# One pass per tile, or three phases over all tiles: reordering an encoder layer with streamed weights

## The chip, the cores and the metric

The kernel runs on all 8 cores of one Trainium2 chip (two dies of four cores). Every core runs the same program on its own share of the data, and no core waits for another. The time of a run is the device time of the slowest core, in microseconds (us). A trace covers one execution; its "span" is the time from a core's first to its last instruction, and the page of a kernel shows its slowest core.

Executions come in two states. In the fast state all cores have nearly the same granted TensorE clock (in the fast runs of the changed kernel, 0.987 to 0.992). In the slow state the cores of one die, sometimes of both, have a lower clock and run longer: where a kernel gave fast runs too, its slow runs in a batch are 1.8 to 17% above the fastest of them. Fast runs are compared with fast runs only; where a kernel gave none, an undisturbed die is compared with an undisturbed die, and the text says so.

Engine names: PE is the matrix engine, PEld its weight load (it overlaps PE: in a window of 100 us of before, 45.32 us of it with PE busy for 99.88), DVE the vector engine, ACT the scalar engine, SP the engine that issues most transfers. "L414" is line 414 of the kernel that is being shown; the line numbers of an experiment can be one off from those of the kernel it was made from.

## The reference, cut to what matters

```python
D_MODEL, D_FF, BATCH, SEQ = 1024, 2816, 16, 2048     # 2 prompt sequences per core
DEC_BATCH, DEC_SEQ = 8, 64                            # 1 sample of 64 tokens per core

def encoder_layer(x, cache_k, cache_v, state_gla, ...):
    h = x + 0.5 * swiglu_ffn(rms_norm(x, norm_ffn1), w_ffn1_in, w_ffn1_out)      # FFN 1
    n = rms_norm(h, norm_mix)
    q_a, k_a, v_a, r_a, f_a, q_b, k_b, v_b, g_a, g_b = split_projection(n, w_in)
    o_a, s_new = gla_branch(q_a, k_a, v_a, r_a, f_a, ...)     # 4 heads, recurrent over chunks of 64
    o_b = band_attention(q_b, k_b, v_b, ...)                  # 16 heads of 64, own chunk + 8 before
    mixed = sigmoid(g_a) * (o_a @ w_branch_gla) + sigmoid(g_b) * (o_b @ w_branch_att)
    h = h + mixed @ w_out
    h = h + 0.5 * swiglu_ffn(rms_norm(h, norm_ffn2), w_ffn2_in, w_ffn2_out)      # FFN 2
    return h, ...                                             # and the new keys, values, GLA state
```

All weights come in as fp32 and are used as bf16. Both kernels cut a core's 4096 prompt tokens into 8 tiles of 512. Each tile needs the GLA state and the last 512 keys and values of the tile before it in its sequence. The sample tile (64 tokens) starts from given caches.

## The kernel before

It takes one tile through the whole layer, then the next; the sample is the last tile. All weights are first cast from fp32 to bf16 by transfers from HBM to HBM (`wsc`), and every tile streams them from there in 1 MB blocks through a ring of three slots.

```python
if not ws.planning and not DIRECT0:                       # at the start: cast all blocks HBM -> HBM
    for j in range(ws.nbt):
        ...
            S.op("pool", (lambda e, d=dst_j, s_=src_j: e.dma_start(out=d, in_=s_)), writes=[("wsc", j)], dma=True)
...
# getw(): a tile's next block of weights, 2 blocks ahead, for every tile anew
S.op("sp", (lambda e, slot=slot, jb=jb, n_el=n_el: e.dma_start(out=ring[:, slot, 0:n_el], in_=wsc[jb][:, 0:n_el])),
     reads=[("wsc", jb)], writes=[("wring", slot)], dma=True)
```

The order of instructions is the order in which the code emits them. In a tile: FFN 1, norm with transposes, projections, GLA, attention, gates and output, norm, FFN 2. Attention takes a head's scores (five matmuls of 64 rows by 128 columns), adds the bias, takes exp, and multiplies by the values (five matmuls of 65 columns); scores of the next head fill PE while ACT and DVE work on this one, and nothing else does.

```python
ins = e.matmul(outp, lhsT=kbT[pb0:pb0 + 64, c, sl * 128:sl * 128 + nk],             # L875, scores
               rhs=qbT[pb0:pb0 + 64, c, s * 128:s * 128 + TP], start=True, stop=True)
... # L881 bias add on DVE; L889 and L895 exp on ACT
ins = e.matmul(acc[:TP, acol:acol + 65], lhsT=Pb[:nk, pbuf, i, 0:TP], rhs=vaug[:nk, sl, hd, :],   # L921, times values
               start=(n_ == 0), stop=(n_ == len(blks) - 1))
...
for q in range(NSEQ):
    for t in range(NT):
        tile("p", q, t)
tile("s", 0, 0)
```

The code makes two readers of one PSUM bank wait for each other (`if kname(r) == "ps": war.add(rd)`). The changed kernel keeps that rule, so it is not part of the difference.

The softmax here doesn't subtract the row's maximum and nothing guards it: scores larger than these inputs give would overflow.

Of the kernel before, what the change touches and what calls it, by code (L numbers as in the profile page):

```python
# [6 lines left out]
F32 = mybir.dt.float32  # L7
# [6 lines left out]
PW = 8208  # L14
EPS = 1e-6
NCORES = 8

COMPUTE = ("pe", "act", "dve")
QUEUES = ("sp", "pool")
NDMASEM = 12  # L20

OVERLAPS = {
    "gT": ["ebT", "enbT", "la", "oaT", "obT", "qdT", "kiT"],
    "ebT": ["gT", "oaT"], "oaT": ["gT", "ebT"],
    "enbT": ["gT", "obT"], "obT": ["gT", "enbT"],
    "la": ["gT", "qdT", "kiT"], "qdT": ["gT", "la"], "kiT": ["gT", "la"],
    "dke": ["oa", "h2"], "oa": ["dke", "h2"], "va": ["ob", "h2"], "ob": ["va", "h2"], "h2": ["dke", "oa", "va", "ob"],
    "hout": ["rr", "qbT"], "rr": ["hout"], "qbT": ["hout"],
    "Pb": ["Pbg"], "Pbg": ["Pb"],
}  # L30

def kname(k):
    return k[0] if isinstance(k, tuple) else k

class Sched:
    def __init__(self):
        self.ops = []
        self.last_w = {}
        self.readers = {}
        self.nseq = {e: 0 for e in COMPUTE + QUEUES}  # L40
        self.pending = {}

    def enter(self, name):
        deps = set()
        others = set(OVERLAPS[name])
        for k, v in self.last_w.items():
            if kname(k) in others:
                deps.add(v)
        for k, v in self.readers.items():
            if kname(k) in others:  # L50
                deps.update(v)
        best = {}
        keep = set()
        for d in deps:
            o = self.ops[d]
            if o["dma"]:
                keep.add(d)
            else:
                if o["eng"] not in best or self.ops[best[o["eng"]]]["seq"] < o["seq"]:
                    best[o["eng"]] = d  # L60
        keep.update(best.values())
        self.pending[name] = keep

    def op(self, eng, fn, reads=(), writes=(), dma=False):
        idx = len(self.ops)
        raw = set()
        war = set()
        for r in reads:
            if r in self.last_w:
                raw.add(self.last_w[r])  # L70
            if kname(r) == "ps":
                for rd in self.readers.get(r, ()):
                    war.add(rd)
        for w in writes:
            if w in self.last_w:
                raw.add(self.last_w[w])
            for rd in self.readers.get(w, ()):
                war.add(rd)
            p = self.pending.get(kname(w))
            if p:  # L80
                raw.update(p)
        for r in reads:
            self.readers.setdefault(r, []).append(idx)
        for w in writes:
            self.last_w[w] = idx
            self.readers[w] = []
        seq = self.nseq[eng]
        self.nseq[eng] += 1
        self.ops.append(dict(eng=eng, fn=fn, raw=raw, war=war - raw, dma=dma, seq=seq,
                             sig=False, waits=[], idx=idx))  # L90
        return idx

    def barrier(self, eng, deps):
        idx = len(self.ops)
        seq = self.nseq[eng]
        self.nseq[eng] += 1
        self.ops.append(dict(eng=eng, fn=None, raw=set(deps), war=set(), dma=False, seq=seq,
                             sig=False, waits=[], idx=idx))
        return idx

    def analyze(self):
        ops = self.ops
        seen = {e: {x: -1 for x in COMPUTE} for e in COMPUTE + QUEUES}
        seen_dma = {e: set() for e in COMPUTE + QUEUES}
        dma_count = {q: 0 for q in QUEUES}
        dma_hist = {q: [] for q in QUEUES}
        for o in ops:
            e = o["eng"]
            deps = [(d, True) for d in sorted(o["raw"])] + [(d, False) for d in sorted(o["war"])]
            if o["dma"]:  # L110
                n = dma_count[e]
                dma_count[e] += 1
                o["dsem"] = n % NDMASEM
                o["dval"] = 16 * (n // NDMASEM + 1)
                if n >= NDMASEM:
                    deps.append((dma_hist[e][n - NDMASEM], True))
                dma_hist[e].append(o["idx"])
            for d, is_raw in deps:
                a = ops[d]
                if a["dma"]:  # L120
                    if d in seen_dma[e]:
                        continue
                    o["waits"].append(d)
                    seen_dma[e].add(d)
                else:
                    ae = a["eng"]
                    if a["fn"] is None:
                        continue
                    if ae == e and ae == "pe":
                        continue  # L130
                    if seen[e][ae] >= a["seq"]:
                        continue
                    o["waits"].append(d)
                    a["sig"] = True
                for x in COMPUTE:
                    if a["vc"][x] > seen[e][x]:
                        seen[e][x] = a["vc"][x]
            vc = dict(seen[e])
            if e in COMPUTE:
                vc[e] = o["seq"]  # L140
            o["vc"] = vc
        cnt = {e: 0 for e in COMPUTE}
        for o in ops:
            if o["eng"] in COMPUTE and o["sig"]:
                cnt[o["eng"]] += 1
                o["sval"] = cnt[o["eng"]]

    def emit(self, sems, dsems, block):
        ops = self.ops
        per = {e: [o for o in ops if o["eng"] == e] for e in COMPUTE + QUEUES}  # L150

        def run(engname, eng):
            for o in per[engname]:
                for d in o["waits"]:
                    a = ops[d]
                    if a["dma"]:
                        eng.wait_ge(dsems[a["eng"]][a["dsem"]], a["dval"])
                    else:
                        eng.wait_ge(sems[a["eng"]], a["sval"])
                if o["fn"] is None:  # L160
                    continue
                ins = o["fn"](eng)
                if o["dma"]:
                    ins.then_inc(dsems[engname][o["dsem"]], 16)
                elif o["sig"]:
                    ins.then_inc(sems[engname], 1)

        block.tensor(lambda eng: run("pe", eng))
        block.scalar(lambda eng: run("act", eng))
        block.vector(lambda eng: run("dve", eng))  # L170
        block.gpsimd(lambda eng: run("pool", eng))
        block.sync(lambda eng: run("sp", eng))

class NullSched:
    def op(self, *a, **k):
        return 0

    def enter(self, name):
        pass

NSLOT = 3
LOOKAHEAD = 2
DIRECT0 = False

class WStream:
    def __init__(self, ring):
        self.ring = ring
        self.plan = []
        self.rearr = []
        self.planning = True  # L190
        self.issued = 0
        self.taken = 0
        self.S = None

    def view(self, slot, shape):
        a, b = shape
        return self.ring[:, slot, 0:a * b].rearrange("p (a b) -> p a b", a=a)

class StopEmit(Exception):
    pass  # L200

def build(NSEQ, SEQLEN, debug=(), stop_at=None):
    nc = bass.Bass("TRN2", target_bir_lowering=False)
    NTOK = NSEQ * SEQLEN
    NT = SEQLEN // 512

    def din(name, shape, dt=F32):
        return nc.dram_tensor(name, shape, dt, kind="ExternalInput").ap()

    def dout(name, shape):  # L210
        return nc.dram_tensor(name, shape, F32, kind="ExternalOutput").ap()

    def dscr(name, shape):
        return nc.dram_tensor(name, shape, BF16, kind="Internal").ap()

    xp = din("xp", [NTOK, D])
    xsm = din("xs", [64, D])
    ck = din("ck", [512, D])
    cv = din("cv", [512, D])
    st = din("st", [4, 128, 256])  # L220
    wsrc = dict(
        w1i=din("w1i", [D, 2 * DFF]), w1o=din("w1o", [DFF, D]), win=din("win", [D, PW]),
# [3 lines left out]
    gnf_d = din("gnf", [1, D])  # L226
    biasT_d = din("biasT", [128, 16, 2, 128])
    cb_d = din("cb", [128, 16])
    consts_d = din("consts", [128, 4, 128])

    yp = dout("yp", [NTOK, D])
    ys = dout("ys", [64, D])
# [953 lines left out]
```

## Time and profile before

| before | value | where read |
|---|---|---|
| time, 3 runs | 5112.84 us median (5000.71 to 5132.51; two of the three are over 2% above the fastest) | runs |
| span, slowest core | 4992.2 us | page |
| PE / DVE / ACT busy | 84% / 29% / 29% | page |
| dense stage | 216 ns per matmul of 512 columns (464 in 100.32 us), clock 1.00 | chain of waits, windows |
| attention stage | 74 us per tile, clock 0.50 | windows |
| a prompt tile | 526 to 591 us | first FFN 1 activation of each tile |
| sample tile | about 240 us (232.6 from its first activation to the end) | the same, to the end |

The lines of the page of before. First busy time with share of the span and number of instructions; then 40 equal slices of the span, each digit the busy share in tenths ("PEclk" is the granted clock in tenths); then the chain of work that ended last, by engine.

```profile
span 4992.2 us, 66123 instructions; the slowest of 8 cores (4942.5 to 4992.2 us)
PE 4201.9 (84%) x22747; PEld 2087.6 (42%) x22747; DVE 1450.3 (29%) x2982; ACT 1444.3 (29%) x2840; POOL 138.9 (3%) x205
...
PE   4646776998999899988999799989999899969956
...
PEclk8778678996999689996999799987999699977975
DMA  9999899430443134330443134322342044322586
...
PE 66%; DMA 14%; another core or an unknown queue 6%; DVE 5%; issue 4%; ACT 3%; POOL 1%; DVEq 0%; ACTq 0%; POOLq 0%; SPq 0%
```

PE looks busy, but PEclk is below 9 in 19 of the 40 slices: at the start, and then once or twice per tile. The first seven slices (the casting) have DMA at 8 tenths or more and PE at 4 to 7 tenths.

Windows of before, core 7: a dense stage and the attention stage of the same tile. Columns are the window, its length, busy time and count per engine, then granted clock, DMA share, GB/s.

```profile
core 7: us, PE busy (x) PEld busy (x) DVE busy (x) ACT busy (x) POOL busy (x), PEclk, DMA share, GB/s
1442.00:1542.00 100.00, 99.88 (x463) 45.32 (x464) 23.87 (x35) 14.99 (x25) 4.32 (x8) 1.00 0.51 174
1688.00:1762.00 74.00, 67.85 (x657) 49.12 (x656) 42.28 (x153) 60.35 (x129) 0.00 (x0) 0.50 0.01 2
```

A line of the chain of waits of before: 464 dense matmuls back to back, 216 ns each.

```profile
1442.12 100.32 PE ps L414 x464
```

### The profile page before, as it was taken

Reading aid. Unit: us, or ns where it says so; the run is one execution under the profiler, and the core shown is the slowest. Engines: PE = TensorE matmul, PEld = TensorE weight load, DVE = VectorE, ACT = ScalarE, POOL = GpSimd, SP = SyncE. Lnnn points to the kernel's source line nnn. Section 1 sums busy time; section 2 is a strip of 40 time slices with the busy share of each in tenths; the row PEclk is TensorE's granted clock in tenths of the full one; section 3 lists DMA queues with packets and bytes.
Section 4 is the critical chain, followed back from the end, with each engine's and each line's share of the span. In section 5 each row is a group of like instructions: output and inputs, shape, how many; then the busy total and the mean of one; then the engine's idle time right before and its main releaser. Section 6 shows DMA issues by size and latency. Waiting matters only on the chain.

```text
span 4992.2 us, 66123 instructions; the slowest of 8 cores (4942.5 to 4992.2 us)
## 1 busy us (share of the span) xinstructions
PE 4201.9 (84%) x22747; PEld 2087.6 (42%) x22747; DVE 1450.3 (29%) x2982; ACT 1444.3 (29%) x2840; POOL 138.9 (3%) x205
## 2 busy tenths in 40 slices
PE   4646776998999899988999799989999899969956
PEld 1222432445444544435444444445444544435434
DVE  2011421225322432215321532234222432134212
ACT  1011411136222532226222422234123622234122
POOL 1100010000000000000000000000000000000000
PEclk8778678996999689996999799987999699977975
DMA  9999899430443134330443134322342044322586
GB/s 148 151 109 126 108 171 170 168 115 22 152 165 121 44 119 150 137 125 24 152 165 115 50 135 164 119 80 97 131 169 102 31 149 163 118 79 79 143 273 218
DMA packets 186614, 631.18 MB, mean 126 GB/s; under 512 B 22417, under 2 KB 110002, under 8 KB 126258
## 3 DMA queue, kind: packets, MB, share of 16 engines
q1 hardware_dynamic: 79570, 539.60, 31.7%
q0 software_dynamic: 106720, 87.36, 14.6%
q8 instruction: 191, 3.13, 0.2%
q14 instruction: 133, 1.09, 0.1%
HBM read 659.21 MB, written 85.25 MB: 149 GB/s over the span
## 4 chain that ended last, share of the span: by engine, by line
PE 66%; DMA 14%; another core or an unknown queue 6%; DVE 5%; issue 4%; ACT 3%; POOL 1%; DVEq 0%; ACTq 0%; POOLq 0%; SPq 0%
PE ps L414 57%; PE ps L875 5%; DMA wsc<-w2i 3%; DMA wsc<-w1i 3%; DMA wsc<-win 3%; PE ps L921 3%; DMA s_ring<-wsc 2%; DVE s_xnT L449 1%; PE ps L438 1%; DMA wsc<-w2o 1%; DVE s_U L828 1%; DMA wsc<-w1o 1%; DMA vpo<-s_ystage 1%; DMA kpo<-s_ystage 1%
## 5 line engine op out<-in xcount | busy, mean ns | idle before, releaser
L414 PE MATMUL ps<-s_xnT,s_ring 128*128 128x512 bf16 (+1 forms) x9216 | 1934.9, 372 | 254.2 <-DMA s_ring<-wsc 184.3
L414 PEld LDWEIGHTS ps<-s_xnT,s_ring 128*128 128x128 bf16 x9216 | 866.7, 103 | 1287.8 <-issue 378.8
L414 PE MATMUL ps<-s_ring,s_UG 128*128 128x512 bf16 (+1 forms) x2904 | 653.3, 387 | 50.1 <-DMA s_ring<-wsc 50.0
L508 DVE TENSOR_TENSOR s_UG<-ps,s_tmpf 128x512 bf16<-128x512 f32 (+1 forms) x396 | 252.2, 640 | 1073.1 <-PE ps L414 1007.0
L414 PE MATMUL ps<-s_ring,s_xnT 128*128 128x512 bf16 (+1 forms) x1992 | 466.6, 395 | 86.1 <-DMA s_ring<-wsc 53.1
L506 ACT ACTIVATE s_tmpf<-ps 128x512 f32<-128x512 f32 (+1 forms) x396 | 218.6, 555 | 1067.2 <-PE ps L414 1034.1
L414 PEld LDWEIGHTS ps<-s_ring,s_UG 128*128 128x128 bf16 (+1 forms) x2904 | 289.2, 100 | 407.9 <-issue 82.3
L875 PE MATMUL ps<-s_U,s_kbT 64*128 64x128 bf16 (+2 forms) x2320 | 333.4, 302 | 52.7 <-DVE s_UG L449 31.6
L414 PEld LDWEIGHTS ps<-s_ring,s_xnT 128*128 128x128 bf16 (+1 forms) x1992 | 200.1, 101 | 352.2 <-issue 142.2
L889 ACT ACTIVATE s_Pb<-ps,s_cbs 128x384 bf16<-128x384 f32 (+3 forms) x464 | 253.8, 547 | 42.8 <-PE ps L875 26.0
L414 PE MATMUL ps<-s_UG,s_ring 128*128 128x512 bf16 (+1 forms) x1152 | 255.1, 367 | 0.3 <-ACT s_UG L445 0.3
L881 DVE SCALAR_TENSOR_TENSOR s_tmpf<-ps,s_biasT 128x256 f32<-128x256 f32 (+1 forms) x528 | 219.4, 418 | 119.2 <-PE ps L875 105.2
L875 PEld LDWEIGHTS ps<-s_U,s_kbT 64*128 64x128 bf16 (+1 forms) x2320 | 201.0, 129 | 106.5 <-issue 62.5
L921 PE MATMUL ps<-s_vaug,s_Pb 128*128 128x65 bf16 (+2 forms) x2320 | 224.0, 242 | 24.0 <-ACT s_Pb L895 18.4
L895 ACT ACTIVATE s_Pb<-s_tmpf 128x256 bf16<-128x256 f32 (+1 forms) x528 | 213.2, 405 | 66.0 <-DVE s_tmpf L881 32.6
L438 PE MATMUL ps<-s_identb,s_xb 128*128 128x128 bf16 (+1 forms) x792 | 85.6, 277 | 145.0 <-ACT s_xb L472 144.1
L921 PEld LDWEIGHTS ps<-s_vaug,s_Pb 128*128 128x128 bf16 (+2 forms) x2320 | 142.4, 124 | 123.4 <-issue 120.1
L455 ACT ACTIVATE s_junk<-s_h 128x1024 bf16<-128x1024 f32 (+1 forms) x34 | 35.9, 1057 | 439.1 <-DVE s_h L529 335.7
L414 PEld LDWEIGHTS ps<-s_UG,s_ring 128*128 128x128 bf16 x1152 | 109.7, 103 | 126.1 <-issue 9.1
L529 DVE SCALAR_TENSOR_TENSOR s_h<-ps,s_U 128x512 f32<-128x512 f32 (+1 forms) x66 | 45.6, 691 | 316.8 <-PE ps L414 316.8
L438 PEld LDWEIGHTS ps<-s_identb,s_xb 128*128 128x128 bf16 (+1 forms) x792 | 66.6, 124 | 169.6 <-issue 167.9
L414 PE MATMUL ps<-s_ring,s_mixT 128*128 128x512 bf16 (+1 forms) x528 | 120.2, 390 | 17.6 <-DVE s_mixT L996 12.7
(119 smaller groups left out, 2510.3 us busy)
## 6 DMA issues: line engine op xcount, KB each, us to landing
s_ring<-wsc SPq DMA_DIRECT2D x468, 1024.0 KB, 5.3
s_ring<-wsc SPq DMA_DIRECT2D x36, 768.0 KB, 4.2
s_U<-xp SPq DMA_DIRECT2D x32, 512.0 KB, 8.2
yp<-s_ystage POOLq DMA_DIRECT2D x64, 256.0 KB, 3.8
wsc<-win POOLq DMA_DIRECT2D x12, 1024.0 KB, 219.2
wsc<-w1i POOLq DMA_DIRECT2D x22, 512.0 KB, 10.7
wsc<-w2i POOLq DMA_DIRECT2D x22, 512.0 KB, 9.7
wsc<-w1o POOLq DMA_DIRECT2D x4, 1024.0 KB, 45.4
```

Of the source, the lines that this page charges most:

```text
L414: ins = e.matmul(out_ap, lhsT=l, rhs=r, start=(start and i == 0), stop=(stop and i == n - 1))
L438: ins = e.transpose(out=pb_[:, k * 128:k * 128 + TP], in_=src_ap[:, k * 128:(k + 1) * 128], identity=identb[:TP, :TP])
L449: S.op("dve", lambda e: e.tensor_tensor(out=dst3, in0=src3, in1=g3, op=ALU.mult), reads=[("ps", b), "gains"], writes=[dstkey])
L506: S.op("act", (lambda e, bg=bg, tb=tb: e.activation(out=tmpf[:, tb, 0:T], in_=bank(bg)[:, 0:T], func=AF.Silu)), reads=[("ps", bg)], writes ...
L508: S.op("dve", (lambda e, bu=bu, tb=tb, j=j: e.tensor_tensor(out=gT[:, j, 0:T], in0=bank(bu)[:, 0:T], in1=tmpf[:, tb, 0:T], op=ALU.mult)), ...
L529: S.op("dve", (lambda e, hv=hv, dv=dv, b=banks[s]: e.scalar_tensor_tensor(out=dv, in0=bank(b)[:TP, :], scalar=0.5, in1=hv, op0=ALU.mult, o ...
L828: S.op("dve", (lambda e, hh=hh, obank=obank, ocol=ocol: e.scalar_tensor_tensor(out=oa[:TP, s, hh * 256:(hh + 1) * 256], in0=obank[:TP, oco ...
L875: ins = e.matmul(outp, lhsT=kbT[pb0:pb0 + 64, c, sl * 128:sl * 128 + nk], rhs=qbT[pb0:pb0 + 64, c, s * 128:s * 128 + TP], start=True, stop ...
L881: S.op("dve", lambda e: e.scalar_tensor_tensor(out=tmpf[:, tb, 0:256].rearrange("p (b q) -> p b q", b=2)[:, :, 0:TP], in0=bank(bB)[:, 0:25 ...
L889: S.op("act", lambda e: e.activation(out=Pb[:, pbuf, i0:i0 + ncst, 0:TP], in_=bank(bA)[:, i0 * 128:(i0 + ncst) * 128].rearrange("p (b q) - ...
L895: S.op("act", lambda e: e.activation(out=Pb[:, pbuf, 3 + i3:5, 0:TP], in_=tmpf[:, tb, 0:256].rearrange("p (b q) -> p b q", b=2)[:, i3:2, 0 ...
L921: ins = e.matmul(acc[:TP, acol:acol + 65], lhsT=Pb[:nk, pbuf, i, 0:TP], rhs=vaug[:nk, sl, hd, :], start=(n_ == 0), stop=(n_ == len(blks) - 1))
```

## The change

The intent: keep PE on dense work all the time. Three phases take the place of eight passes. FFN 1 runs for all tiles with its weights cast straight into SBUF, once, and kept; the mixer runs for all tiles with streamed blocks of weights, and the small matmuls of GLA and attention are spread among the dense matmuls of the same and of the next tile; FFN 2 runs for all tiles with its weights kept. The weights of the mixer and of FFN 2 are cast in the background. Features lie on partitions, so no norm needs a transpose: squares are summed over partitions by one fp32 matmul with ones (512 columns). Sigmoids are made of exp and ln. The residual goes through HBM between the phases. The sample shares the weight blocks of tile 0 in the mixer.

An order of instructions is no longer written by hand. Every operation gets a due time, and a list scheduler places it by modelled durations. The diff is a rewrite (some 3,000 lines); this is its core, with cuts:

```diff
-for q in range(NSEQ):
-    for t in range(NT):
-        tile("p", q, t)
-tile("s", 0, 0)
+def ld_w1(i, due, after=()):                     # fp32 HBM -> bf16 SBUF, kept for the whole phase
+    return dma(due, "pool", view(W1 + 4096 * i, 2048), w1i[i], 1 << 20, w=[(("W1", i), 1)], after=after, tag="w1")
+for hf in range(2):                              # x of tile 0 in halves, the second after the first
+    lx.append(dma(0.002 + 5.5 * hf, "sp", xv_of("X0", 512)[:, :, hf * 256:(hf + 1) * 256], ..., lx[-1:], tag="ldx"))
+...
+seq1 = [(2, 512, "X0"), (3, 512, "X1"), ..., (6, 512, "X0"), ("S", 64, "XS"), (7, 512, "X1")]
+t = run_ffn(t, seq1, src1, 1, None)              # FFN 1, all tiles
+...
+tc0, tc1 = TT[(1, 2)] - 60.0, TT[(1, "S")]       # background casts of the mixer weights
+for i in range(22):
+    conv(tc0 + (tc1 - tc0) * i / 22, wmb[i], wmx[i], 3 << 20, [(("wmb", i), 0)], "cvm")
+...
+# the mixer: dense stages of tile n mixed with stages of tile n - 1
+stages += [("2", n), ("gb", n - 1), ("wo", n - 1), ("1", n), ("ga", n)]
+gla(tiles[n], span[("2", n)][1] + 0.1, span[("1", n)][1] - 2.0)
+attention(tiles[n], mid("1", n, 0.8), mid("2", n + 1, 0.93), NUNIT)   # spread over due times
+...
+run_ffn(t_mix_end, seq2, src2, 2, None)          # FFN 2, all tiles, then the sample
```

In the changed kernel L692 is the dense matmul, L1557 the scores, L1597 the exp, L1623 the product with the values.

## The prediction

> **What bounds the kernel now.** The page of before: span 4992 us, PE busy 84%, DVE and ACT 29% each. The chain of waits puts 57% on the dense matmul line, 14% on DMA. The windows show four regimes:
>
> 1. [...] The chain shows 464 matmuls of 512 columns in 100.32 us (216 ns each); granted clock 1.00 on all eight cores. [...]
> 2. GLA and attention (1660 to 1764 us): 104 us of small matmuls, clock 0.55, nothing dense to fill in. Norms with transposes (1543 to 1560): PE half idle, clock 0.70. A prompt tile takes 542 us (1442 to 1984); its 1815 dense matmuls account for 392, so 150 us are such stages.
> 3. Start: the first tile ends near 1003 us instead of about 540. DMA is 85 to 100% busy until 900 us, casting weights HBM to HBM; the chain is all "wsc". About 460 us lost.
> 4. End: the 64-token sample tile streams all weights again (4745 to 4992 us), 247 us for little PE work.
>
> **What the change does.** FFN weights are cast once into SBUF and stay for all tiles; mixer and FFN 2 weights are cast in the background. The sample rides with the first mixer tile. Features lie on partitions, so norm transposes vanish, replaced by squares and one fp32 ones-matmul (about 1 us, as the 128x512 fp32 matmul took). Attention and GLA are interleaved with dense work of the same and next tile. Sigmoids go through exp/ln: ACT about 115 us and DVE about 100 us per mixer tile by durations of before (0.6 and 0.69 us per 512 columns, 1.02 per 1024), under PE's 195. HBM round trips of h bring DMA to about 140 GB/s, below the 300 the sample tile reached.
>
> **Cost.** PE floor from the instruction list, [...] 34 ns at least (32 matmuls of 64 columns took 1.09 us), fp32 fourfold: FFN 1 953 us, mixer 1520, FFN 2 974, sum 3447. Added, estimates: start 15, waits for first weights 10 to 20 (6.9 us per 0.5 MB needed; the casting queue moved some 105 GB/s of bf16, 5 us), mixer bubbles 6% (90), phase changes and tail 30, launch beside span 8. About 3605 us. All of it is on the critical path: PE is the chain.
>
> **What would show it.** FFN phases: PE 99% busy, clock 1.00, weight DMA only in the first 200 us. Mixer: clock above 0.95, PE over 90%, gaps under 1 us, 200 us per tile. No weight waits after the start; no sample stage of 250 us.
>
> **What would make it wrong.** (a) [...] Before's runs (5001 to 5133) already look like two states. (b) The order is fixed from modelled durations; where ACT or DVE run longer (three-step sigmoids, bias adds, scans), PE stalls: 10% more in the mixer is 150 us. (c) Casts below 76 GB/s delay the first two tiles.
>
> Predicted: 3605 us, 8 in 10 between 3500 and 3800. Faster by over 2%: 0.98; within 2%: 0.01; slower: 0.01.

The floor came to 3447 us (953 + 1520 + 974), the additions to 158 (15 + 15 + 90 + 30 + 8), in all 3605. The traces give 216.2 ns per 512 columns (464 in 100.32 us in before), 0.11 us for 256 (1684.10 to 1684.21 in before), 0.45 us for eight of 128 (1906.75 to 1907.20 in after), and 0.86 us for the fp32 matmul of 512 (1570.15 to 1571.01 in before), four times 0.216. The 34 ns for 64 columns come from before; in after 40 matmuls of 65 columns took 1.21 us (1836.82 to 1838.03), 30 ns each. The 105 GB/s are the best stretch of the casting queue (2.15 MB from 840 to 860 us); over the first 885 us it moved 57.73 MB, 65 GB/s. The 76 GB/s of (c) are an estimate: 0.5 MB in 6.9 us, the time of 32 matmuls at 216 ns. (a), the premise that long dense work lowers the clock, was the fear, and no run had shown it. Regime 1 is the dense stages.

## More of the kernel before

In attention PE is counted busy for 67.85 of 74 us, more than nine tenths, and yet the granted clock is half. The timeline of before inside that stage (start, duration, what) shows one head after the other:

```profile
1742.16 0.71 PE L875 MATMUL ps<-s_U,s_kbT 64*128 64x128 bf16 x5
1742.46 0.42 ACT L895 ACTIVATE s_Pb<-s_tmpf 128x256 bf16<-128x256 f32 x1
...
1742.81 0.46 PE L921 MATMUL ps<-s_vaug,s_Pb 128*128 128x65 bf16 x5
1742.97 0.58 ACT L889 ACTIVATE s_Pb<-ps,s_cbs 128x384 bf16<-128x384 f32 x1
...
1743.19 0.71 PE L875 MATMUL ps<-s_U,s_kbT 64*128 64x128 bf16 x5
```

A head takes 1.03 us (1743.19 less 1742.16). ACT's two exps of a head last 0.58 and 0.42 us, together nearly as long as a head.

## The result, and the profile after

The changed kernel took 3648.47 us (median of four: 3643.38, 3640.94, 3653.56, and a slow run of 4154.92; the mean of the three fast ones is 3646.0), before 5056.77 in the same rounds. The ratio is 0.7289, with a 95% interval of 0.7251 to 0.7327. The record takes a ratio from fast runs alone, so it is not the ratio of the medians quoted.

The same lines of the page of after:

```profile
span 3641.8 us, 55773 instructions; the slowest of 8 cores (3618.3 to 3641.8 us)
PE 3478.3 (96%) x20446; PEld 1647.3 (45%) x20446; DVE 1578.4 (43%) x2928; ACT 1374.1 (38%) x2427; POOL 98.6 (3%) x297
...
PE   7998999998999999999999999999899999999998
...
PEclk9999999999999999999999999999999999999999
DMA  9344433442534363636555453536641001110100
...
PE 85%; DMA 5%; ACT 4%; DVE 4%; issue 2%; SPq 0%; DVEq 0%; ACTq 0%; POOL 0%; POOLq 0%
```

The clock is now nine tenths or more in every slice. Windows of after, core 6: most of FFN 1, the place where the sample is put into FFN 1, the mixer, and most of FFN 2.

```profile
core 6: us, PE busy (x) PEld busy (x) DVE busy (x) ACT busy (x) POOL busy (x), PEclk, DMA share, GB/s
300.00:880.00 580.00, 572.74 (x2640) 256.73 (x2638) 189.57 (x292) 142.94 (x224) 9.33 (x19) 1.00 0.35 77
880.00:985.00 105.00, 92.78 (x836) 51.21 (x833) 42.58 (x91) 33.02 (x71) 14.28 (x9) 0.92 0.47 102
1060.00:2630.00 1570.00, 1494.09 (x10473) 730.99 (x10472) 884.48 (x1801) 850.47 (x1563) 54.47 (x225) 0.99 0.51 161
3000.00:3600.00 600.00, 593.11 (x2716) 265.17 (x2715) 200.12 (x306) 149.31 (x233) 0.00 (x0) 1.00 0.08 32
```

The FFN windows have PE busy for 98.7% and 98.9% at full clock; the mixer has 95% at 0.99. A piece of the mixer in the timeline of after, PE only, shows how attention is spread:

```profile
1831.82 0.61 PE L1557 MATMUL ps<-sb 64*128 64x256 bf16 x8
1832.36 3.63 PE L692 MATMUL ps<-sb 128*128 128x512 bf16 x16
1836.28 0.61 PE L1557 MATMUL ps<-sb 64*128 64x512 bf16 x4 [0.29 <-ACT sb L1597]
1836.82 1.38 PE L1623 MATMUL ps<-sb 128*128 128x65 bf16 x40
1838.03 1.89 PE L692 MATMUL ps<-sb 128*128 128x512 bf16 x8
```

Between two groups of scores lie 3.6 us of dense work. When the values are due, exp has long been done, or nearly: in the mixer (1060 to 2630 us) the product with the values waited for exp five times, 1.2 us at the longest.

**Where the time went.** Two accounts of the same time. The first goes by parts of the program (core 7 of before, core 6 of after; boundaries from the first FFN activation of each tile, so good to some 5 us; the 195 of a mixer tile is from the run without the sample, where six of them took 195.6 on average). It closes only by its last row:

| part | before | after | saved |
|---|---|---|---|
| start | first tile ends at 885; a later tile takes 552 on average: 333 lost | about 55 lost (57.6 us until PE is back to back, with 23 us of work done by then, an estimate from the count of matmuls; and a stop near 280) | 278 |
| 8 prompt tiles | 552 each | 118 + 195 + 118 = 431 each | 968 |
| sample | 242 | 105 (run without it, below) | 137 |
| edges between phases, tail | | | -33 (the rest) |
| span | 4992 | 3642 | 1350 |

The second goes by the granted clock. The trace has a record of each stretch at one clock; summed over the execution (the records cover all but some 20 to 43 us of a span; each core is the slowest of its run):

| kernel, core | us at half clock | us at full clock |
|---|---|---|
| before, 7 | 1416.9 | 3532.8 |
| after, 6 | 89.9 | 3522.3 |
| a_onetile, 6 (overlap within a tile only) | 286.4 | 3522.6 |
| a_noint, 7 (no overlap) | 803.8 | 3440.6 |

The time at full clock hardly differs between before and after, 3533 and 3522 us. What vanished is the time at half clock, 1327 of the 1350 us. In before it lies in several places: 365 us in the first 885, 171 in the sample tile, and the whole of every full attention stage (74 us each). This is a correlation, not yet a cause: PE works at half clock in stages in which it is starved (in the first 885 us it is busy for 548.70), and also in attention, where it is counted busy (67.85 of 74 us). The experiments take that apart.

### The profile page after: what moved, and what is told of

Its sections match the earlier page's. It is cut to its first block, busy times and chain, and to the rows that moved or that the text cites. A ratio compares the mean times of both kernels' runs of the same rounds, so it can differ in the third digit from the quotient of the medians.

```text
span 3641.8 us, 55773 instructions; the slowest of 8 cores (3618.3 to 3641.8 us)
## 1 busy us (share of the span) xinstructions
PE 3478.3 (96%) x20446; PEld 1647.3 (45%) x20446; DVE 1578.4 (43%) x2928; ACT 1374.1 (38%) x2427; POOL 98.6 (3%) x297
## 3 DMA queue, kind: packets, MB, share of 16 engines
q0 software_dynamic: 17824, 59.97, 10.5%
## 4 chain that ended last, share of the span: by engine, by line
PE 85%; DMA 5%; ACT 4%; DVE 4%; issue 2%; SPq 0%; DVEq 0%; ACTq 0%; POOL 0%; POOLq 0%
PE ps L692 78%; PE ps L1557 2%; PE ps L1623 2%; DMA h2d<-sb 1%; DMA sb<-h1d 1%; ACT sb L1597 1%; DMA h1d<-sb 1%; PE ps L721 1%; DVE sb L737 1%; ACT L762 1%; DMA sb<-xT 1%; DVE sb L1140 1%; DVE sb L765 0%; DMA vpo<-sb 0%; PE ps L1652 0%
## 5 line engine op out<-in xcount | busy, mean ns | idle before, releaser
L692 PE MATMUL ps<-sb 128*128 128x512 bf16 (+3 forms) x15384 | 3201.4, 367 | 99.7 <-DVE sb L765 23.2
L692 PEld LDWEIGHTS ps<-sb 128*128 128x128 bf16 (+1 forms) x15384 | 1412.8, 99 | 1772.0 <-issue 216.3
L765 DVE TENSOR_TENSOR sb<-ps,sb 128x512 bf16<-128x512 f32 (+2 forms) x400 | 252.8, 634 | 826.6 <-PE ps L692 752.9
L762 ACT ACTIVATE sb<-ps 128x512 f32<-128x512 f32 (+2 forms) x400 | 219.7, 551 | 824.8 <-PE ps L692 745.8
L712 ACT ACTIVATE sb<-sb 128x512 f32<-128x512 f32 (+1 forms) x245 | 140.5, 584 | 476.4 <-DVE sb L775 444.7
L1597 ACT ACTIVATE sb<-ps 128x1024 bf16<-128x1024 f32 (+1 forms) x288 | 274.6, 992 | 115.2 <-DVE ps L1588 113.5
L714 DVE TENSOR_TENSOR sb<-sb 128x512 f32<-128x512 f32 (+1 forms) x245 | 155.9, 637 | 112.3 <-ACT sb L712 103.9
L737 DVE SCALAR_TENSOR_TENSOR sb<-sb 128x512 bf16<-128x512 f32 (+3 forms) x280 | 174.1, 692 | 62.3 <-ACT sb L726 62.3
L1588 DVE TENSOR_TENSOR ps<-ps,sb 128x512 f32<-128x512 f32 (+1 forms) x304 | 167.6, 593 | 76.3 <-PE ps L1557 74.3
L681 DVE CAST sb<-ps 128x512 bf16<-128x512 f32 (+4 forms) x174 | 119.0, 684 | 120.6 <-PE ps L692 116.3
L1115 ACT ACTIVATE sb<-sb 128x512 f32<-128x512 f32 (+1 forms) x202 | 124.5, 616 | 15.5 <-ACT sb L1114 0.4
L1117 ACT ACTIVATE sb<-sb 128x512 f32<-128x512 f32 (+1 forms) x202 | 124.1, 614 | 14.1 <-ACT sb L1115 0.4
L1557 PE MATMUL ps<-sb 64*128 64x256 bf16 (+3 forms) x896 | 86.5, 300 | 9.0 <-ACT sb L1597 8.9
L1623 PE MATMUL ps<-sb 128*128 128x65 bf16 x2240 | 79.9, 195 | 10.4 <-ACT sb L1597 5.8
L1623 PEld LDWEIGHTS ps<-sb 128*128 128x128 bf16 x2240 | 75.1, 98 | 31.4 <-issue 25.1
L707 ACT ACTIVATE sb<-sb 128x512 f32<-128x512 f32 (+1 forms) x35 | 20.4, 583 | 125.7 <-DVE sb L775 122.9
## 6 DMA issues: line engine op xcount, KB each, us to landing
wmb<-wmx POOLq DMA_DIRECT2D x22, 1024.0 KB, 10.7
h1d<-sb SPq DMA_DIRECT2D x8, 2048.0 KB, 18.9
```

The costliest lines, as they stand in the source:

```text
L692: ins = e.matmul(o_, lhsT=l() if callable(l) else l, rhs=r_() if callable(r_) else r_, start=(i == 0), stop=(i == m - 1))
L712: act(due, lambda e: e.activation(out=sq, in_=view(xo, T, F32), func=AF.Square), c_act(T, True), [(xp, xi)], [((sqs, b), (inst, k))], tag= ...
L714: dve(due + 0.01, lambda e: e.tensor_tensor(out=acc, in0=acc, in1=sq, op=ALU.add), c_dve(T), [((sqs, b), (inst, k)), (accn, (inst, k - 1)) ...
L737: dve(due, lambda e: e.scalar_tensor_tensor(out=dst, in0=view(xo, T, F32), scalar=gains[:, g, k:k + 1], in1=RR, op0=ALU.mult, op1=ALU.mult ...
L762: act(due + 0.02, lambda e: e.activation(out=tm, in_=bank(pg)[:, 0:T], func=AF.Silu), c_act(T), [pg], [(fp, ti)], tag="silu")
L765: dve(due + 0.03, lambda e: e.tensor_tensor(out=G, in0=bank(pu)[:, 0:T], in1=tm, op=ALU.mult), c_dve(T), [pu, (fp, ti)], [((gp, i), d)], t ...
```

## The experiments

The theory (A): most of the gain comes from mixing GLA and attention with dense work, so that their chain of waits and their low clock cost nothing. Rivals: (B) the gain comes from weights that stay on chip; (C) from the start and the sample; (D) the mixer would be as fast with attention alone, since the changed layout has larger matmuls there.

Twelve kernels were run in three batches, each on one chip with runs of before beside it. Fast runs only, in us:

| kernel | edit | fast runs | fast runs of before in the batch |
|---|---|---|---|
| a_noint | after, attention and GLA alone on PE | 4264.69 | 4997.89, 4999.9, 5000.44 |
| a_onetile | after, overlap within a tile only | 3829.11 | same |
| a_hdouter | after, scores by head | 3642.64, 3643.53, 3643.97 | same |
| a_restream | after, FFN 2 weights loaded for every tile | 3653.39, 3651.83 | same |
| b_filler | before, 1 dense matmul per head | 5160.01 | 5019.29, 5024.48, 5073.32 |
| b_5banks | before, 5 score banks (control) | 5034.84 | same |
| b_direct0 | before, first tile casts into SBUF | 4963.93 | same |
| b_nosample | before without the sample | none | same |
| b_filler4 | before, 4 dense matmuls per head | 5187.18 | 4998.98, 5003.7, 5010.21, 5026.62, 5029.9 |
| a_nosample | after without the sample | 3538.77 | same |
| a_convlate | after, later casts | 3635.93, 3639.26, 3640.68, 3642.89 | same |
| a_best | a_convlate, and a faster first load | 3623.84, 3628.55, 3632.2, 3633.54, 3636.31 | same |

a_hdouter turned out to equal after (below), so it serves as after in the first batch. Seven of the kernels gave a single fast run; what they show is read from differences that are large beside the spread of the others, or from their traces.

### a_noint and a_onetile: taking the overlap away

```diff
+GAPS = {"2": 50.0, "1": 90.0}                    # a_onetile: {}
-stages += [("2", n), ("gb", n - 1), ("wo", n - 1), ("1", n), ("ga", n)]
+stages += [("2", n), ("1", n), ("ga", n), ("gb", n), ("wo", n)]
+# a_noint: GLA and attention fall into the gaps; PE work of one stage waits for all of the stage before
+for k in range(1, len(grp)):
+    for o in grp[k]:
+        o.deps.update(grp[k - 1])                # a_onetile: only where ga ends and where a tile ends
```

> The changed kernel, but in the mixer the GLA and the attention of a tile each run alone on the PE, as in the kernel before (barriers on PE only; same instructions, same results). Theory A (the dense work laid under attention and GLA is what the mixer gains): the two stages then last as long as ACT and DVE need, estimated 28 us for GLA and 45 to 55 us for attention a tile, against the 39 us of PE time that they take interleaved; 3950 to 4100 us, and the granted clock in those stretches falls below 0.8. Rival B (the gain is in the cheaper form of attention, two heads a bank pair and wider instructions, and the interleaving adds little): at most 80 us more than 3643, clock unchanged.

> The changed kernel, interleaving kept inside a tile (GLA under the q/k/v projections of attention, attention under their tail and under the GLA branch's gates), but no work of tile n+1 starts before tile n has ended, and the attention branch's gates wait for attention. Theory A with the overlap of tiles as its main part: halfway, 100 to 250 us over 3643. If within-tile overlap is enough: within 60 us of 3643. If overlap does not matter at all (B): no change.

a_noint took 4264.69 us, 621 more than after (a_hdouter's mean of 3643.4 in the same batch). a_onetile took 3829.11, 186 more. The FFN phases did not move: the last tile of FFN 1 begins at 914.0 us in the trace of a_noint and at 914.6 in after, the second tile of FFN 2 begins 621 us later than in after, and both run 118 us per tile. So the loss lies in the mixer. Window of a_noint, core 7, one attention stage by itself:

```profile
2014.00:2104.00 90.00, 41.40 (x486) 26.75 (x485) 32.78 (x75) 43.41 (x49) 6.81 (x33) 0.63 0.15 42
```

PE is busy less than half of it, at a clock of 0.63. The stage takes 89 us, GLA alone 29 (both from the timeline of PE); spread over dense work the two cost their matmul time only, an estimate of 39 us from the instruction list. That gives 89 + 29 - 39 = 79 us for a full tile; the trace has 279 to 285 us for a full mixer tile against 191 to 203 in after. (The first tile of a sequence has fewer keys: 243 us.) Rival D falls. The loss is larger than expected, since attention by itself takes longer than was thought: scores, bias add, exp and the product with the values wait for each other, and PE stands for up to 3.7 us at a time. That more PSUM banks for scores would shorten this was not tried.

Note what this run does not say. Alone, the changed kernel's attention is slower than that of before (89 against 74 us), so the 621 us are what the overlap is worth in the changed kernel, not a share of the 1350. Against before's own stages (104 us for GLA and attention of a full tile, 1660 to 1764 us) the overlap is worth 104 - 39 = 65 us per full tile, an estimate.

a_onetile shows that the tile's own dense work doesn't suffice, at least as it is scheduled there. The waits of PE in the mixer of a_onetile (in all, times, longest):

```profile
PE ps L1556 <- ACT sb L1596: 96.1, 55, 3.7
```

and the wait for the same exp in the mixer of after:

```profile
PE ps L1557 <- ACT sb L1597: 8.9, 13, 1.6
```

So theory A is shown in the changed kernel, but not its "most of the gain": the overlap carries 621 us, of which 186 are lost already when work of the next tile may not be mixed in. By the account above, rival C holds some 415 of the 1350 us (278 at the start, 137 for the sample). The part of the sample is supported by two runs below; what in the change saves the time at the start was not tried by itself.

### a_restream: are kept weights worth much?

```diff
-rw = [(("W1", i), ph)]
+rw = [(("W1", i), ph if ph == 1 else (2, d[1]))]
+for (n, T, buf), (pn, pT, pb) in zip(seq2[1:], seq2[:-1]):     # every tile of FFN 2 loads W1 and WO again
+    for i in range(22):
+        dma(TT[(2, pn)] + 16 * c_mm(pT) * i + 0.1, "sp", view(W1 + 4096 * i, 2048), w2ib[i], ...)
```

> The changed kernel with FFN 2's weights loaded again from HBM for each tile (17 MB a tile, bf16), in place of kept. Theory: keeping them is not what makes the FFN phases fast, as the kernel before streamed them at 216 ns a matmul with clock 1.00; time within 15 us of 3643, an FFN 2 tile still 118 us, DMA share there 0.3 to 0.5 in place of under 0.1. Rival: the loads make PE wait, or traffic slows PE: 3 us or more a tile, 25 us or more in all.

It cost 9 us (3652.6 against 3643.4). A tile of FFN 2 took 119.4 us instead of 118. Window of a_restream, core 5:

```profile
3000.00:3600.00 600.00, 585.86 (x2675) 262.01 (x2673) 197.10 (x301) 148.52 (x231) 0.00 (x0) 1.00 0.51 176
```

DMA is at 0.51 (expected up to 0.5) instead of 0.08, and PE at 97.6% instead of 98.9%. Rival B falls for FFN 2: loading the weights anew for every 512 tokens hides behind PE. "Weights kept on chip" is in the headline of the change, and is worth a quarter of a per cent there. What it buys in FFN 1, casting straight into SBUF at the start, was not tried by itself.

### a_hdouter: the order of score matmuls

```diff
-for (c_, u) in grp:
-    for (j, s0, ns, c0) in units[u]:
-        ...
-        for hd in range(2):
+for hd in range(2):
+    for (c_, u) in grp:
+        for (j, s0, ns, c0) in units[u]:
```

> The changed kernel with the score matmuls (64 rows each) issued all of head 0, then all of head 1, in place of alternating. Theory: two matmuls on different halves of the array's rows run at once when they alternate (the profile shows 86.5 us busy for 286,720 columns[...]); ordered by head that is lost[...], time 20 to 40 us longer as PE is the limit. Rival: the order makes no difference, the busy time of the profile is only its model; no change of time beyond 10 us.

Scores use 64 rows where dense matmuls use 128 (64*128 and 128*128 in the trace), and the order in after alternates the upper and the lower half. That two such matmuls run together was the inference from after's busy time: 86.5 us for the line's 286,720 columns, which at 216 ns per 512 take 121 us one after another, an estimate. If alternating them were what lets them run together, this edit would lose it. Ratio 0.7288 (0.7271 to 0.7304) against 0.7289: no change. In the trace 224 score matmuls of 512 columns took 39.9 us busy here and 39.4 in after. The traces say why: the overlap is there in both. A group of four in a_hdouter:

```profile
1833.80 0.61 PE L1557 MATMUL ps<-sb 64*128 64x512 bf16 x4 [0.27 <-ACT sb L1597]
1834.35 1.38 PE L1623 MATMUL ps<-sb 128*128 128x65 bf16 x40
```

The next matmul starts 0.55 us after the first score, as in after (1836.28 to 1836.82, above); at 216 ns each, four matmuls of 512 columns one after another need 0.86. Start by start, the score matmuls come in 448 pairs of one width in both traces, the two of a pair 4 ns apart in after (median) and 13 ns here. So score matmuls do overlap in after, and the order by head does not prevent it. The packed trace doesn't say which half a matmul used: that a pair is an upper and a lower half was not shown, and how the order by head still comes out in pairs stays open.

### b_filler, b_5banks, b_filler4: what holds the clock down in before?

In before PE is counted busy in attention for 92% of the time at clock 0.50. If the clock follows the density of work, which is the theory here, dense matmuls put among the heads would raise it. They write to a spare bank; nobody reads it.

```diff
-POOLS = {..., "C": [0, 1, 2, 3, 4, 5], "D": [6, 7]}
+POOLS = {..., "C": [0, 1, 2, 3, 4], "D": [6, 7]}                      # this alone: b_5banks
+mmgroup(bank(5)[:, 0:512], [(xnT[:, 0, 0:128], xnT[:, 1, 0:512])], nkeys, [("ps", 5)])          # b_filler
+mmgroup(bank(5)[:, 0:512], [(xnT[:, 0, 0:128], xnT[:, 1, 0:512])] * 4, nkeys, [("ps", 5)])      # b_filler4, instead
```

> The kernel before with one dense 128x512 matmul, whose result nobody reads, put ahead of each head's scores in attention (512 in the prompt tiles), and five score banks instead of six to make room. Theory A: attention is limited by ACT (0.58 + 0.41 us of exp a head, 1.03 us a head measured), PE is slow there only because its clock has dropped; the fillers keep the clock up (0.55 to over 0.9 in this stage) and cost nothing: time within 40 us of the kernel with five banks and no filler. Rival B: PE is the limit of that stage (it is 80 to 100% busy), so each filler adds its 0.22 to 0.43 us: 110 to 220 us more.

> Control for the filler run: the kernel before with five score banks instead of six, no filler. Both theories: within 1% of the kernel before, clock in attention still about 0.55.

b_5banks took 5034.84, within before's 5019.29 to 5073.32. b_filler took 5160.01, 125 more than b_5banks. It adds 528 matmuls (64 heads in each of 8 tiles, and 16 of the sample), 114 us at 216 ns. So on the whole the filler was not free (each number is one fast run; the fast runs of before differ by 54 us); theory A's number was missed, and the 125 lie in rival B's range. The trace shows why, and it is neither theory. Its profiled run was slow on one die, so this is read on the other, undisturbed one (clock 0.860 to 0.868). Two attention stages of b_filler, core 7:

```profile
2285.00:2385.00 100.00, 94.28 (x715) 52.83 (x712) 44.11 (x152) 63.36 (x128) 0.00 (x0) 0.51 0.00 1
1708.00:1781.00 73.00, 66.87 (x719) 39.09 (x716) 38.21 (x147) 58.20 (x130) 0.00 (x0) 0.83 0.01 2
```

The same instructions took 100 us in one tile and 73 in another. In the first the clock stayed at half: a head takes 1.46 us, PE back to back. In the second it was full for part of the time, and there a head takes 0.86 us, less than the 1.03 of before, with more work in it. With one dense matmul per head both were seen, 0.51 and 0.83, and which it is differs from tile to tile and core to core (from 1700 to 1800 us, which is not cut to the stage, cores 4, 5 and 6 had 0.87, 0.83 and 0.79).

Four per head were to decide it:

> The kernel before with four dense 128x512 matmuls (instead of the one of b_filler) ahead of each head's scores in attention; they add 448 x 4 x 0.216 = 387 us of work at full clock, 774 at half. In b_filler one dense matmul per head left two kinds of attention stage on undisturbed cores: 100 us at a granted clock of 0.50 (1.46 us per head, PE back to back) and 73 us at 0.83 (0.855 us per head where the clock was full), against 73 to 75 us at 0.50 in before. Theory A (the clock follows how much dense work is in the mix, and attention alone is too thin to lift it although PE is busy): with four per head the clock in the attention stages is above 0.9, a head takes 0.64 + 3 x 0.216 = about 1.5 us, a stage of 64 heads 95 to 110 us, that is only some 25 to 35 us longer than in before for 55 us of added work, and the span grows by 150 to 300 us. Rival B (these stages are held at half clock whatever is mixed in): clock stays near 0.5, a head takes 1.03 + 4 x 0.43 = 2.75 us, a stage about 176 us, and the span grows by 700 us or more.

b_filler4 took 5187.18 us, 173 more than the mean of the fast runs of before in its batch (5013.9). The expectation wrote 448 heads; there are 528, so the added work is 528 x 4 x 0.216 = 456 us at full clock. Two attention stages of b_filler4, core 7:

```profile
1685.00:1786.00 101.00, 100.13 (x903) 49.47 (x904) 41.04 (x147) 63.34 (x130) 0.00 (x0) 0.95 0.01 2
2291.00:2390.00 99.00, 96.63 (x904) 48.27 (x903) 42.67 (x150) 63.15 (x129) 0.00 (x0) 1.00 0.01 2
```

and its timeline:

```profile
1741.22 0.45 PE L875 MATMUL ps<-s_U,s_kbT 64*128 64x128 bf16 x5
1741.60 0.33 PE L922 MATMUL ps<-s_vaug,s_Pb 128*128 128x65 bf16 x5
1741.77 1.03 PE L414 MATMUL ps<-s_xnT 128*128 128x512 bf16 x4
```

In all eight cores (mean clock of the execution 0.923 to 0.929) the full prompt stages ran at 0.95 to 1.00, in 97 to 102 us from the first score matmul to the last. The five score matmuls took 0.45 us instead of 0.71. Such a stage holds 55 us of added work (64 x 4 x 0.216) and is only 24 to 28 us longer than the 73 to 75 of before. Rival B (176 us a stage) falls.

What follows: in before, the half clock of attention is not a matter of PE waiting for long, since PE was nearly back to back there (67.85 of 74 us). In these runs it goes with how little dense work is in the mix: 0.50 with none, 0.51 or 0.83 with one dense matmul per head, 0.95 to 1.00 with four. Attention among dense matmuls, as in after, therefore gains twice: its waits are filled, and its own matmuls run at or near full clock (the mixer window has 95% and 0.99). Over before, 456 us of dense work fit in for 173 (one run). This is the cheapest demonstration of what the rewrite does.

### b_direct0, b_nosample, a_nosample: start and sample

```diff
-DIRECT0 = False
+DIRECT0 = True          # b_direct0: the first tile casts each block into SBUF and stores it to HBM from there
-order = [...] + [("s", 0, 0)]
+order = [...]           # b_nosample; outputs of the sample are left unwritten, wrong on purpose
-tile("s", 0, 0)
```

> The kernel before with the first tile's weights cast from HBM straight into the SBUF ring and stored to HBM as bf16 from there (a switch the kernel has). Theory: the first tile's 460 us of excess come from the cast HBM to HBM and reading back, at 70 to 105 GB/s of bf16 written; straight into SBUF the cast ran at some 130 GB/s in the changed kernel's first 100 us, so 200 to 350 us less. Rival: the start is bound by the casting queue's rate wherever it writes, so less than 80 us saved.

4963.93 us (one fast run) against 5019.29 to 5073.32, so 55 to 109 less; the mean of before gives 75. (The run of 5073.32 counts as fast, but one die has a clock of 0.841 to 0.848 in it; without it the mean gives 58.) In the trace the first FFN 1 stretch of the second tile begins at 854.39 us instead of 903.23, 49 earlier. The first tile still takes some 284 us too long (333 - 49). The size is the rival's (below 80 us): the start of before isn't mended by saving one trip through HBM. That the rate of the casting queue is what binds it, as the rival has it, was not shown.

> The kernel before without the 64-token sample tile (its outputs are wrong on purpose). Theory: the sample tile is bound by streaming all weights once more, so the time falls by its whole stage, 230 to 265 us. Rival: part of it hides under the last prompt tile's end; under 200 us.

All four runs were slow on one die. On the undisturbed die the cores took 4716 to 4767 us, those of before in the same batch on undisturbed dies 4964 to 5026: about 250 less. This agrees with the some 240 us that the sample tile takes in before's trace.

> The kernel after without the sample tile (its outputs are left unwritten, wrong on purpose). In before, leaving it out saved about 250 us. Theory A (the sample rides on weights that are there anyhow, and costs only its own small matmuls: 1120 of 128x64, 43 us busy in the page, plus its attention, GLA and edges): 50 to 110 us less than after. Rival B (the sample keeps a stage of its own in which PE starves): 200 us or more less.

The edit takes the sample out of `seq1`, of the mixer's stages and of FFN 2; its outputs are unwritten. One fast run, 3538.77; spans 3516.9 to 3537.2 against 3618.3 to 3641.8. So the sample costs 105 us (3641.8 - 3537.2) in after, at the upper end of what was expected. In the trace without it, FFN 1 ends 36 us earlier (the last store of h is issued at 997.9 us instead of 1033.9), FFN 2 begins 86 us earlier, so some 50 lie in the mixer, and the remaining 19 us are its FFN 2 part at the end. In FFN 1 the price is some twice the work (528 matmuls of 34 ns, 18 us, an estimate with the 1.09 us of before for 32 matmuls of 64 columns): there the window from 880 to 985 us of after, above, has PE idle for 12 us and a clock of 0.92, and the chain of waits there goes through the lines of the next tile's norm. That 64 tokens are too short to cover that norm is argued from this, not tried.

### a_convlate and a_best: the two stops at the start

From the chain of waits of after, the first 330 us (start, duration, what):

```profile
57.63 138.40 PE ps L692 x640
...
235.48 26.91 DMA h1d<-sb
262.45 10.79 DMA sb<-xT
...
290.40 33.14 PE ps L692 x144
```

PE is back to back from 57.6 us on. At 278 it stops again: the third tile's x may be loaded only when the first tile's h, in the same buffer, has been stored, and that store took 26.9 us, while the background casts of the mixer weights began.

```diff
-tc0, tc1 = TT[(1, 2)] - 60.0, TT[(1, "S")]
+tc0, tc1 = TT[(1, 2)] + 20.0, TT[(1, "S")]                            # a_convlate and a_best
-    ..., 1 << 20, (), [(("X0", k), ("x", 0)) for k in range(8)], lx[-1:], tag="ldx"))
+    ..., 1 << 20, (), [(("X0", k), ("x", 0)) for k in range(8)], (), tag="ldx"))      # a_best only
```

> The kernel after with the background casts of the mixer weights begun 80 us later in FFN 1. Theory A (PE's stop at 278 to 290 us comes from the store of the first tile's h, which took 26.9 us because the casts share the DMA engines, and which holds back the load of the third tile's x): the stop goes, with the 17 us of half clock beside it, and the time falls by 8 to 20 us (0.2 to 0.5%); the store takes under 15 us. Rival B (the store is slow by itself or the stop only moves): change below 4 us.

> a_convlate, and the second half of the first x tile no longer waits for the first half to land (in after the halves landed at 13.1 and 22.3 us, the first FFN matmul began at 26.5, and PE was back to back from 57.6). Theory A (the wait between the halves costs time at the start): both halves land by 19 us, PE is back to back before 52 us, and the time is 4 to 10 us below a_convlate. Rival B (the start is bound by the bytes of x and W1 at some 175 GB/s, in whatever order): within 3 us of a_convlate.

In a_convlate the store in question took 16.7 us instead of 26.9 (issued at 234.5, and the load that waits for it at 251.3), and the median of all eight stores of h fell from 18.9 to 8.9. Between 250 and 300 us PE was busy for 42.98 us at clock 0.93, where after had 37.59 at 0.83. So the casts cost that store some 10 us. (In after the five later stores of h that met a cast took 15.7 to 19.5 us, the last two, which met none, 8.6 and 10.7; 2 MB each.) It still missed the 15 expected: the first cast was issued only at 306.2 us, so what is left is not theirs; a load of x ran beside it (233.7 to 244.9). And the stop became shorter, it did not go: PE now waits there for norms (the chain names DVE). Later, at 415 and 533 us, it was loads of x that met the casts, and took 18.2 and 20.5 us instead of 11.0 and 10.1: part of the collision was only moved. The mean of the fast runs is 3639.7; after had 3646.0 on another chip, with runs from 3640.9 to 3653.6. A gain of some 6 us is less than the 8 to 20 expected, and with two chips it can't be told from none.

a_best was run beside a_convlate: mean 3630.9, 8.8 us less, as expected. The first half of x landed at 15.5 us and the second at 18.2, instead of 13.0 and 21.8 in after; here are the beginnings of the unbroken PE work, first of a_convlate (core 6), then of a_best (core 1):

```profile
56.79 138.29 PE ps L692 x640
```

```profile
51.80 136.57 PE ps L692 x632
```

5 us of the gain are seen there. a_best has a ratio of 0.7236 (0.7214 to 0.7258) to before; all of its five fast runs are below all fast runs of after and of a_hdouter, though on other chips. It is the fastest version, by about 0.4%.

## Why the prediction was right

The time was predicted at 3605 us, between 3500 and 3800, and was 3648. The main step was right: after is bound by PE, and its time is the sum of PE's matmul work at full clock plus small losses. The floor in the prediction was 3447, so 201 us were lost, where the prediction's additions sum to 158. That the two lie so close is in part luck: one addition was some 50 us too small and one some 27 too large. The phases of after (core 6) are told apart here by counting dense matmuls, since the first of FFN 2 are mixed with the last of the mixer: FFN 1 ends at 1034 us, and at 2664.6 as many are left as FFN 2 has. Point by point:

- **FFN 1: mis-sized.** The floor was 953 us; the phase took 1034, so 81 over, where "start 15, waits for first weights 10 to 20" make some 30. The start itself was right: PE was back to back at 57.6 us with 23 us of work done, 35 lost. Left out were the stop at 278 us (about 20, with the half clock after it) and the sample's place between two tiles (36 us for some 18 of work); the rest, some 8, is about 1 us per tile. a_best took back a part of this.
- **Mixer: nearly right, the loss was a little under-estimated.** 1520 was the floor, 1631 was measured: 111 us, or 7%, against the predicted 90, or 6%. In the window of 1570 us above PE stood for 76. The order from modelled durations held: the largest wait of PE for exp was 1.6 us, the largest of all 3.8 (for a DVE add, L1341).
- **FFN 2 and the tail: the addition was not needed.** 974 was the floor, 977 measured; 30 were foreseen for phase changes and tail.
- **The fear of a lower clock under long dense work: not borne out in the fast runs.** All fast runs of after had 0.987 to 0.992 on every core, and the trace has at most 10.5 us at a clock between half and full (0.8125) on any core. In slow runs one die is lower: the slow run of a_convlate of 4261.57 us had 0.811 on the cores of die 1; that of after had 0.835 to 0.837 on die 0 and took 4154.92. So dense work for 3.6 ms does not bring on the low clock in every run, but in the runs that have it after and its variant lose 14 and 17%.
- **What the profile should show.** PE at 99% and clock 1.00 in the FFN phases: 98.7 and 98.9%, 1.00. Mixer above 0.95 and 90%: 0.99 and 95%. "Gaps under 1 us": not quite, they reach 3.8. A mixer tile 200 us: 191 to 203. "Weight DMA only in the first 200 us": no, the casts of the mixer weights run from 216 to 863 us (DMA share 0.35), and their collision with a store made the stop at 278 longer.
- **A misreading.** The prediction said that the first tile of before ends near 1003 us, and that 460 us were lost at the start. The first FFN 1 activation of the second tile comes at 890 us; 1003 is the end of that tile's first dense stretch. The loss was about 333. The predicted time did not use this number, so nothing followed from it there; the expectation of b_direct0 still used it.
- **GLA and attention as a stage of 104 us with clock 0.55, "nothing dense to fill in":** the reading was right, and b_filler4 shows for attention that four dense matmuls per head lift the clock from 0.50 to 0.95 to 1.00. The prediction did not say that the low clock is there even where PE is back to back; the runs show that (b_filler: PE busy for 94.28 of 100 us at 0.51).

What stays open: what decides the clock in attention (b_filler's two kinds of stage for one program); how the 968 us of the prompt tiles split between the overlap and the rest (transposes, norms, stores, and the cheaper form of attention's matmuls), which were not tried one by one; what of the change saves the 278 us at the start; and why one die at times falls into the slow state.

## What to carry to other kernels

Look at the granted clock per stage, not only at the busy share: a stage of thin matmuls can be counted over 90% busy and run at half the clock (67.85 of 74 us at 0.50 in before), and enough dense work mixed into it can cost less than half its own length (173 us for 456 in b_filler4), while too little did not pay (125 for 114 in b_filler). Reordering a program so that thin, latency-bound stages of one tile lie among the dense stages of another was worth 621 us in the changed kernel, while keeping weights on chip in FFN 2, which the reordering also allowed, was worth 9. When such a kernel is bound by PE at full clock, predict it from the matmul list, and look for the error at the start and at the seams, where short tiles and shared transfers make the stops.
